# Moving transposes and row statistics of V, K, Q, HGRN input and convolution further behind their producers in a two-layer hybrid trunk

## The chip, the core and the metric

The kernel runs on one core of a Trainium2 chip. The metric is the device time of one execution in microseconds (us); a result is the median of several executions. The engines are named as in the profile: PE is the matrix engine (PEld is its weight load), DVE the vector engine, ACT the scalar engine, POOL the general-purpose engine, SP the engine whose queue issues the transfers.

## The reference, cut to what matters

```
for l in range(2):
    h = rms_norm(x, norm_mix[l])
    z = h @ w_in[l]                                   # 20 blocks of 128 columns
    q_a, k_a, v_a, q_h, i_h, f_fw, f_bw, g_h, a_c, g_c = split(z)
    q_a, k_a = rope(rms_norm(q_a, q_norm[l])), rope(rms_norm(k_a, k_norm[l]))
    o_att = block_attention(q_a, k_a, v_a)            # 8 query heads, 2 key heads of 64
    o_hg  = hgrn2_bidirectional(q_h, i_h, f_fw, f_bw, g_h, ...)
    o_cv  = conformer_conv(a_c, g_c, ...)             # GLU, 31 taps, layer norm, swish
    x = x + concat(o_att, o_hg, o_cv) @ w_out[l]
    x = x + square(relu(rms_norm(x) @ w1[l])) @ w2[l]
```

All is float32, 1024 tokens of 1024 features.

## The kernel before, in words

Activations lie with features on the partitions and the 1024 tokens along the row. A dense product of one block of 128 output columns ("a column" below) is made in `dense_steps` (L214): eight steps over the input blocks, each of six matmuls of 128x512 (three passes of a split into a high and a low part, for two halves of the tokens). The columns come in the order of ZORDER. A column's result stands in a pair of PSUM banks, the tile S, of which there are two; smaller results go to banks `c` and `e`, two of each. `evac` (L316) multiplies the result by the row's 1/rms into SBUF on DVE.

A layer goes through these stages:

1. The four convolution columns, then five columns for HGRN half 0: `Hgrn(0)` computes gates and, last, the input `iv` from column 8, which it transposes on PE at once (L438 to L445, into the tile `vt`).
2. `h0.core()` (L510), the recurrence of half 0 as a generator: `near` (L447), one multiplication, then for six levels `scores` (L476) and a multiplication, then the transposes of K into `Kt` (L532), the states `U` (L545), the outputs `o` (L562) and the output norm. It has 29 yields. At each yield the loop at L702 draws `qg, cg, qg, cg`: two steps of `qkv` (the six columns V, K, Q0 to Q3) and two steps of `conv_all`, whose 60 taps are single DVE instructions (L352), 30 for each of two halves, with `conv_tail` (L366) behind them.
3. `Hgrn(1)` with five more columns; between them it draws three more steps of the convolution, and ahead of its last column it makes the scores of the first two attention units. `drain(cg)` ends the convolution.
4. 64 attention units (the loop over `u`, L828): scores into S, scaling and row extreme on DVE (L756), exponential on ACT (L759), the normalisation on POOL (L761), eight transposes on PE (L782), a copy on ACT (L786) and a subtraction on DVE (L787) for each half, and the products with V (L803). `h1.core()`, the recurrence of half 1, is drawn once every second unit. When it is exhausted, the mixed results are read back and split (L205, L206).
5. The output columns, then the two MLP products, each made of seven block products with fewer multiplications.

The parts of `qkv`: `vpart` evacuates V, and after its yield makes eight transposes (L637). `kpart` evacuates K and squares it; after its yield come the row sums on PE (`tok_sums`, L162), a reciprocal root on DVE (`rstd`), a spread to full rows on ACT (`widen`, L168), the rotary steps (`rope`), eight transposes of the spread factors (`flip`, L178), two multiplications (L660) and the store to `kd`. `qpart` squares and scales on ACT straight from S and does the rest, up to the store to `qd`, after its yield. The rest of each part is run when the next column is at its third step:

```
                for k, _ in enumerate(zsteps(col, lambda zp: start(part(zp)))):
                    if k == 2 and rest:
                        drain(rest.pop(0))
                    yield
```

`conv_tail` has two halves, a mean and a variance; each is a chain of `tok_sums`, `widen`, `flip` and four multiplications or subtractions on DVE (L379, L394), and it ends with a scaling on POOL (L397), a sigmoid on ACT (L398), a product on POOL (L399) and the store.

What sets the order: every engine has its own queue, which it works through in order. The framework fills the queues when it compiles: the order of the program is the priority, and an instruction that its model of the times holds for not ready is passed by later ones that are. A `yield` therefore gives the work that is drawn at that place the precedence over what stands behind the yield. Tiles of one tag share a fixed number of buffers, and the next tile waits for the release of an old one: `x8` has 8, `tmp` has 4, `X` and `T` of the HGRN one each (`Kt` takes the buffer of `T`), `m4` five.

Of the kernel before, what the change touches and what calls it, by code (L numbers as in the profile page):

```python
# [17 lines left out]
P = 128  # L18
# [27 lines left out]
def tile_hybrid_trunk(  # L46
# [223 lines left out]
    def drain(gen):  # L270
        for _ in gen:
            pass
# [14 lines left out]
    for l in range(DEPTH):  # L287
# [78 lines left out]
        def conv_tail(ys):  # L366
# [5 lines left out]
            mc = cst.t([P, 8], "mc", bufs=2)  # L372
            nc.vector.tensor_copy(mc, sp[:, 0:8])
            w = widen(mc, 1)
            for h in range(2):
                b = flip(w, h)
                for y in ys:
                    sl = y[:, h * 512 : (h + 1) * 512]
                    nc.vector.tensor_tensor(sl, sl, b, op=ALU.subtract)  # L379
# [7 lines left out]
            sp = pse()  # L387
            tok_sums(sp, sq[0], mean_w)
            w = widen(rstd(sp[:, 0:8], 8, 1.0), 1)
            for h in range(2):  # L390
                b = flip(w, h)
                for y in ys:
                    sl = y[:, h * 512 : (h + 1) * 512]
                    nc.vector.tensor_tensor(sl, sl, b, op=ALU.mult)  # L394
# [7 lines left out]
        class Hgrn:  # L402
            def __init__(self, ls, mid=lambda: None):
# [31 lines left out]
                mid()  # L435
                iv = self.iv = hg.t([P, L], "m4", bufs=5)
                evac(ztile(8 + ls), iv)
                for h in range(2):  # L438
                    tpv = pse()
                    for q in range(4):  # L440
                        c = h * 4 + q
                        nc.tensor.transpose(tpv[:, q * P : (q + 1) * P], iv[:, c * P : (c + 1) * P], ident)
                    nc.scalar.activation(
                        vt[:, h * 4 : h * 4 + 4, :], tpv.rearrange("p (a b) -> p a b", a=4), AF.Copy
                    )  # L445

            def near(self):  # L447
                X, w0, iv = self.X, self.hks, self.iv
# [3 lines left out]
                for hf in range(2):  # L452
# [2 lines left out]
                        op=ALU.mult,  # L455
                    )
                yield
                t = tmp()
                for h in range(2):
                    sl = slice(h * 512, (h + 1) * 512)  # L460
# [49 lines left out]
            def core(self):  # L510
# [23 lines left out]
                for d in range(2):  # L534
                    for g in range(2):
                        tk = psc()
                        for q in range(4):
                            c = g * 4 + q
                            nc.tensor.transpose(tk[:, q * P : (q + 1) * P], X[:, 3 * d, c * P : (c + 1) * P], ident)
                        nc.scalar.activation(  # L540
                            Kt[:, d, g * 4 : g * 4 + 4, :], tk.rearrange("p (a b) -> p a b", a=4), AF.Copy
                        )
                    yield
                for d in range(2):
                    U = pse()  # L545
                    for c in range(8):
# [100 lines left out]
        def kpart(zp):  # L647
# [5 lines left out]
            sp = pse()  # L653
            tok_sums(sp, sq, hsel)
            krw = widen(rstd(sp[:, 0:16], 16, 1.0 / 64), 2)
            nc.gpsimd.tensor_scalar(kz, kz, pv(l, "kn"), 0.0, op0=ALU.mult, op1=ALU.add)
            rope(kz)
            for h in range(2):
                sl = kz[:, h * 512 : (h + 1) * 512]
                nc.vector.tensor_tensor(sl, sl, flip(krw, h), op=ALU.mult)  # L660
# [26 lines left out]
        def qkv():  # L687
            rest = []

            def start(part):  # L690
                rest.append(part)
                next(part)

            for col, part in [(5, vpart), (4, kpart)] + [(j, lambda zp, j=j: qpart(zp, j)) for j in range(4)]:
                for k, _ in enumerate(zsteps(col, lambda zp: start(part(zp)))):
                    if k == 2 and rest:
                        drain(rest.pop(0))
                    yield
            drain(rest.pop(0))

        qg = qkv()
        for _ in h0.core():  # L702
# [125 lines left out]
        for u in range(NU):  # L828
# [5 lines left out]
            if u >= 2:  # L834
                att_values(u // 2 - 1, u % 2)
            att_flip(u, 1)
            if gen is not None and u % 2 == 0:
                try:
                    next(gen)
                except StopIteration:  # L840
# [443 lines left out]
```

## Time and profile before

| | |
|---|---|
| median of 3 runs | 2546.32 us (2542.85 to 2547.26) |
| the profiled execution | 2548.54 us |
| its span in the profile | 2546.8 us |
| PE busy | 2451.1 us, 96% |
| DVE busy | 2003.2 us, 79% |
| ACT busy | 1202.9 us, 47% |
| POOL busy | 779.0 us, 31% |

The profiled execution is 2.22 us over the median, and its span is 1.74 us shorter than its own time. In the views below, the timeline gives start, duration, engine, line, operation, output <- input, and in square brackets how long the engine had been idle and which instruction ended the wait. "x4" merges four instructions in a row. A table of windows gives for each stretch of the span the busy time of each engine and in brackets the number of instructions. The view of waits gives, for an engine and a line, the sum, the number and the longest of its waits for another engine's line.

### The profile page before, as it was taken

The page shows a single profiled execution, that of the slowest core. Times are in us where ns is not written, and L with a number is a line of the kernel's source. Part 1 is how long each engine was busy: PE and PEld are TensorE (multiplying, and loading weights), DVE is VectorE, ACT ScalarE, POOL GpSimd, SP SyncE. Part 2 cuts the span into 40 slices and gives each one's busy share as a digit, 9 for nine tenths or more (in the row PEclk, how much of TensorE's full clock was granted, in tenths as well). Part 3 has the DMA queues.
Part 4 walks back from the last instruction along what each step waited for, and adds up shares of the span by engine and source line. Part 5 has one row for each costly group of instructions (what it writes and reads, how often), then busy time and mean ns, then how long its engine had stood idle before and what let it go on. Part 6 is the DMA issues. An engine that isn't in the chain of part 4 may idle for free.

```text
span 2546.8 us, 34055 instructions
## 1 busy us (share of the span) xinstructions
PE 2451.1 (96%) x12608; PEld 2020.0 (79%) x12608; DVE 2003.2 (79%) x3023; ACT 1202.9 (47%) x1960; POOL 779.0 (31%) x491
## 2 busy tenths in 40 slices
PE   8989999999999999999999899999999999999999
PEld 7767778878778887888887777888787888878887
DVE  5998598872887777987859985898639877789876
ACT  4222478863544443443423225787635444444332
POOL 0232566433154430000123325664331544200000
PEclk9999999999999999999999999999999999999999
DMA  4101310032244448454221113000322444574442
GB/s 157 60 25 63 103 35 18 14 124 96 83 168 158 148 166 302 162 175 152 69 106 50 42 63 104 18 18 26 133 90 95 163 143 167 191 260 155 162 155 91
DMA packets 113077, 286.99 MB, mean 113 GB/s; under 512 B 11408, under 2 KB 11664, under 8 KB 112912
## 3 DMA queue, kind: packets, MB, share of 16 engines
q1 hardware_dynamic: 112912, 284.83, 32.2%
q8 instruction: 99, 1.62, 0.3%
q14 instruction: 66, 0.54, 0.1%
HBM read 197.75 MB, written 87.03 MB: 112 GB/s over the span
## 4 chain that ended last, share of the span: by engine, by line
PE 77%; DVE 14%; ACT 3%; issue 2%; POOL 2%; DMA 1%; SPq 0%; DVEq 0%; ACTq 0%; POOLq 0%
PE S L223 15%; PE S L1195 10%; PE c L995 9%; PE e L1195 7%; PE c L1195 6%; PE e L995 6%; PE S L995 6%; DVE x L352 4%; PE e L803 4%; PE c L782 3%; PE S L745 3%; PE e L494 2%; PE e L162 1%; PE e L583 1%; DVE P L756 1%
## 5 line engine op out<-in xcount | busy, mean ns | idle before, releaser
L223 PE MATMUL S<-xs,whi 128*128 128x512 f32 x1280 | 363.7, 405 | 10.4 <-ACT xs L208 8.9
L223 PEld LDWEIGHTS S<-xs,whi 128*128 128x128 f32 x1280 | 243.3, 193 | 66.2 <-ACT xs L208 8.9
L223 PE MATMUL S<-xs,wlo 128*128 128x512 f32 x640 | 203.3, 398 | 0.0
L1195 PE MATMUL S<-xs,xs 128*128 128x512 f32 x816 | 201.2, 390 | 0.3 <-DVE xs L897 0.3
L896 ACT ACTIVATE xs<-m 128x512 fp32r<-128x512 f32 x216 | 126.0, 619 | 157.4 <-DVE m L907 52.3
L761 POOL TENSOR_SCALAR P<-P,mx 128x1024 f32<-128x1024 f32 x124 | 142.4, 1149 | 162.8 <-DVE mx L760 125.3
L787 DVE TENSOR_TENSOR PT<-c,PT 128x512 fp32r<-128x512 f32 x256 | 171.1, 684 | 23.0 <-ACT PT L786 21.5
L786 ACT ACTIVATE PT<-c 128x512 fp32r<-128x512 f32 x256 | 147.3, 593 | 67.7 <-PE c L782 64.2
L1195 PEld LDWEIGHTS S<-xs,xs 128*128 128x128 f32 x816 | 153.1, 188 | 32.8 <-DVE xs L897 1.2
L199 ACT ACTIVATE whi<-raw 128x1024 fp32r<-128x1024 f32 x56 | 59.1, 1058 | 245.9 <-PE S L223 232.8
L803 PE MATMUL e<-PT,x 128*128 128x256 f32 x1024 | 172.3, 298 | 0.8 <-ACT PT L786 0.5
L756 DVE TENSOR_SCALAR_CACHE_REDUCE P<-S,nqc 128x1024 f32<-128x1024 f32 x124 | 158.6, 1279 | 13.9 <-PE S L745 8.7
L352 DVE SCALAR_TENSOR_TENSOR x<-x,par,x 128x1009 f32<-128x1009 f32 (+14 forms) x120 | 166.7, 1390 | 1.8
L897 DVE TENSOR_TENSOR xs<-m,xs 128x512 fp32r<-128x512 f32 x216 | 144.9, 694 | 24.8 <-ACT xs L896 24.8
L260 POOL TENSOR_TENSOR tmp<-tmp,tmp 128x1024 f32<-128x1024 f32 x19 | 50.6, 2664 | 364.4 <-ACT tmp L259 364.2
L782 PE MATMUL c<-cons,P 128*128 128x128 f32 x992 | 151.9, 277 | 10.5 <-POOL P L761 5.6
L745 PE MATMUL S<-x,QS 128*128 128x512 f32 x480 | 153.8, 419 | 4.9 <-DVE P L756 4.6
L759 ACT ACTIVATE P<-P,mx 128x1024 f32<-128x1024 f32 x124 | 142.5, 1149 | 24.6 <-DVE P L756 23.3
L1195 PE MATMUL e<-xs,xs 128*128 128x512 f32 x552 | 142.9, 395 | 7.2 <-ACT xs L896 6.8
L803 PEld LDWEIGHTS e<-PT,x 128*128 128x128 f32 x1024 | 138.9, 193 | 8.5 <-ACT PT L786 2.2
L782 PEld LDWEIGHTS c<-cons,P 128*128 128x128 f32 x992 | 115.1, 141 | 36.7 <-issue 10.4
L223 PEld LDWEIGHTS S<-xs,wlo 128*128 128x128 f32 x640 | 122.4, 192 | 26.6 <-issue 0.3
(310 smaller groups left out, 5679.3 us busy)
## 6 DMA issues: line engine op xcount, KB each, us to landing
m<-ad SPq DMA_DIRECT2D x104, 512.0 KB, 3.8
ad<-x SPq DMA_DIRECT2D x176, 256.0 KB, 2.1
raw<-w_in_t SPq DMA_DIRECT2D x40, 512.0 KB, 3.3
xs<-w_t SPq DMA_DIRECT2D x36, 512.0 KB, 3.8
raw<-w_t SPq DMA_DIRECT2D x36, 512.0 KB, 3.6
m<-w_t SPq DMA_DIRECT2D x32, 512.0 KB, 6.3
ad<-tmp SPq DMA_DIRECT2D x48, 256.0 KB, 2.2
x<-w_t SPq DMA_DIRECT2D x24, 512.0 KB, 4.8
```

The lines of the kernel that those rows point to most:

```text
L223: nc.tensor.matmul(zp[h] if type(zp) is list else zp[:, h, :], w, xx[:, h * 512 : (h + 1) * 512], start=first, stop=last)
L352: nc.vector.scalar_tensor_tensor(y[:, lo:hi], u[:, lo + d : hi + d], par[:, l, wof + tap : wof + tap + 1], y[:, lo:hi], op0=ALU.mult, op1= ...
L745: nc.tensor.matmul(S[:, hb, :], qs, kk[:, hb * 512 : (hb + 1) * 512], start=first, stop=not first)
L756: nc.vector.tensor_scalar(Pt, S, nqc[:, j, ci : ci + 1], 3.0e38, op0=ALU.mult, op1=ALU.min, accum_out=mx[:, 1:2])
L759: nc.scalar.activation(Pt, Pt, AF.Exp, bias=mx[:, 1:2], scale=-1.0, accum_out=mx[:, 2:3])
L782: nc.tensor.transpose(t[:, q * P : (q + 1) * P], Pt[:, hb, q * P : (q + 1) * P], ident)
L786: nc.scalar.activation(hi, src, AF.Copy)
L787: nc.vector.tensor_tensor(lo, src, hi.bitcast(F32), op=ALU.subtract)
L803: nc.tensor.matmul(pvp[:, cs], VS[g][:, hb * 4 + kb, :], pt[:, kb, :], start=hb == 0 and n == 0, stop=hb == 1 and n == 7,)
L897: ordered("v", nc.vector.tensor_tensor(lo, src, hi.bitcast(F32), op=ALU.subtract))
L995: nc.tensor.matmul(bank, w[i][:, kt * P : (kt + 1) * P], BC[name][kt][j], start=n == 0 and name not in ("M6", "M7", "M3"), stop=n == 11, s ...
L1195: nc.tensor.matmul(banks[dt], w[i][:, dt * P : (dt + 1) * P], a[j], start=n == 0 and name not in ("M6", "M7", "M3"), stop=n == 3 * SG - 1, ...
```

## The change

Six edits, all of the place at which instructions stand in the program; the arithmetic is the same.

- The transposes of `iv` leave the constructor of `Hgrn` and become a generator `turned`, which `near` runs behind two yields, with a yield behind each half. `near` has 6 yields in place of 3. This holds for both halves of the HGRN.
- In the core, the yield behind the transposes into `Kt` stands behind each group of four and not behind two groups: 4 yields in place of 2. The core has 34 yields in all.
- `conv_tail` yields 4 times between `widen` and `flip` of the mean, and 6 times between those of the variance.
- `kpart` has two more yields: ahead of the scaling and rotary steps, and ahead of the transposes.
- `qkv` no longer drains the rest of a part at the third step of the next column. It resumes it once at the seventh step; K, in the column Q0, at the third and fifth; and at every step while two parts are open, which is how the last third of K runs at the first step of Q1.
- The attention loop draws from `h1.core()` at every unit up to 13, and at every second one from 14 on.

```
@@ conv_tail
             w = widen(mc, 1)
+            for _ in range(4):
+                yield
             for h in range(2):
                 b = flip(w, h)
...
             w = widen(rstd(sp[:, 0:8], 8, 1.0), 1)
+            for _ in range(6):
+                yield
             for h in range(2):
                 b = flip(w, h)
@@ Hgrn
                 evac(ztile(8 + ls), iv)
+
+            def turned(self):
                 for h in range(2):
                     tpv = pse()
                     for q in range(4):
                         c = h * 4 + q
-                        nc.tensor.transpose(tpv[:, q * P : (q + 1) * P], iv[:, c * P : (c + 1) * P], ident)
+                        nc.tensor.transpose(tpv[:, q * P : (q + 1) * P], self.iv[:, c * P : (c + 1) * P], ident)
                     nc.scalar.activation(
-                        vt[:, h * 4 : h * 4 + 4, :], tpv.rearrange("p (a b) -> p a b", a=4), AF.Copy
+                        self.vt[:, h * 4 : h * 4 + 4, :], tpv.rearrange("p (a b) -> p a b", a=4), AF.Copy
                     )
+                    yield
@@ near
                 yield
+                yield
+                yield from self.turned()
                 t = tmp()
@@ core
                             Kt[:, d, g * 4 : g * 4 + 4, :], tk.rearrange("p (a b) -> p a b", a=4), AF.Copy
                         )
-                    yield
+                        yield
@@ kpart
             krw = widen(rstd(sp[:, 0:16], 16, 1.0 / 64), 2)
+            yield
             nc.gpsimd.tensor_scalar(kz, kz, pv(l, "kn"), 0.0, op0=ALU.mult, op1=ALU.add)
             rope(kz)
+            yield
             for h in range(2):
@@ qkv
+            def resume(_=None):
+                if rest and next(rest[0], 1) is not None:
+                    rest.pop(0)
+
             for col, part in [(5, vpart), (4, kpart)] + [(j, lambda zp, j=j: qpart(zp, j)) for j in range(4)]:
                 for k, _ in enumerate(zsteps(col, lambda zp: start(part(zp)))):
-                    if k == 2 and rest:
-                        drain(rest.pop(0))
+                    if len(rest) > 1 or k in ((2, 4) if col == 0 else (6,)):
+                        resume()
                     yield
-            drain(rest.pop(0))
+            while rest:
+                resume()
+                yield
@@ attention loop
-            if gen is not None and u % 2 == 0:
+            if gen is not None and (u % 2 == 0 or u < 14):
```

29 lines of the change are left out of this document (22 added, 7 removed).

## The prediction

> **What bounds the kernel now.** I read the page first, then a table of windows that cuts each layer at the stages the change touches, then PE's view of waits, then the timeline around each wait.
>
> The page:
>
> ```profile
> span 2546.8 us, 34055 instructions
> PE 2451.1 (96%) x12608; PEld 2020.0 (79%) x12608; DVE 2003.2 (79%) x3023; ACT 1202.9 (47%) x1960; POOL 779.0 (31%) x491
> ```
>
> PE is idle for 2546.8 - 2451.1 = 95.7 us. The change leaves PE's work as it is, so all that it can win is part of these idle times, and what is won there counts fully only where PE does not meet the next wait at once. The windows, for layer 0 (HGRN half 0 with V, K, Q; HGRN half 1's columns; the first 15 units or so of the attention; its end) and the first three for layer 1:
>
> ```profile
> 62.00:240.00 178.00, 158.73 (x890) 128.64 (x890) 168.77 (x216) 50.10 (x65) 52.78 (x24) 0.95 0.15 54
> 240.00:317.00 77.00, 74.87 (x419) 60.51 (x418) 44.13 (x78) 28.83 (x32) 33.82 (x16) 0.98 0.26 86
> 317.00:372.00 55.00, 49.16 (x316) 40.27 (x313) 52.21 (x92) 42.59 (x76) 36.79 (x26) 1.00 0.14 44
> 540.00:572.00 32.00, 28.61 (x171) 23.62 (x169) 23.22 (x42) 23.65 (x35) 9.29 (x8) 0.95 0.55 194
> 1327.00:1505.00 178.00, 162.91 (x892) 131.28 (x892) 167.49 (x217) 49.98 (x65) 54.71 (x24) 0.93 0.15 51
> 1505.00:1582.00 77.00, 73.79 (x421) 59.52 (x419) 46.96 (x78) 29.45 (x33) 35.16 (x15) 1.00 0.27 87
> 1582.00:1637.00 55.00, 49.97 (x312) 41.47 (x312) 51.06 (x89) 41.34 (x74) 35.50 (x27) 0.97 0.14 43
> ```
>
> The columns are the window, its length, and busy PE, PEld, DVE, ACT, POOL. In the first stage PE idles 178 - 158.73 = 19.3 us in layer 0 and 15.1 us in layer 1, while DVE idles only 9.2 and 10.5 us: DVE is the fuller engine there. In the second stage PE is nearly full and DVE has 32.9 and 30.0 us to spare. At the start of the attention both are near full: PE idles 5.8 and 5.0 us, DVE 2.8 and 3.9 us.
>
> PE's waits, of both layers together (sum, number, longest):
>
> ```profile
> PE e L442 <- DVE m L322: 11.1, 4, 4.3
> PE e L637 <- DVE A L501: 9.8, 2, 6.2
> PE e L178 <- ACT tmp L168: 7.2, 5, 2.8
> PE c L539 <- ACT T L540: 6.1, 2, 3.1
> PE e L494 <- DVE tmp L660: 4.1, 2, 2.1
> PE e L162 <- DVE A L505: 3.3, 2, 2.3
> ```
>
> These six rows are 41.6 us, and they are the transposes and sums that the change moves, or neighbours of them on the two `e` banks. Two in the timeline, the transposes of `iv` and those of V:
>
> ```profile
> 105.92 10.59 DVE L352 SCALAR_TENSOR_TENSOR x<-x,par,x 128x1017 f32<-128x1017 f32 x6
> 106.05 3.40 POOL L432 TENSOR_TENSOR tmp<-tmp,tmp 128x1024 f32<-128x1024 f32 x1 [4.70 <-ACT tmp L429]
> 113.04 0.39 PE L223 MATMUL S<-xs,whi 128*128 128x512 f32 x1
> 116.43 1.22 DVE L322 TENSOR_TENSOR m<-S,Rb 128x1024 f32<-128x1024 f32 x1
> 117.70 1.33 PE L442 MATMUL e<-cons,m 128*128 128x128 f32 x8 [4.27 <-DVE m L322]
> 126.17 1.26 DVE L352 SCALAR_TENSOR_TENSOR x<-x,par,x 128x1011 f32<-128x1011 f32 x1
> 145.50 1.27 DVE L501 TENSOR_TENSOR A<-e,masks 128x512 f32<-128x512 f32 x2
> 146.23 1.97 PE L637 MATMUL e<-cons,tmp 128*128 128x128 f32 x8 [6.23 <-DVE A L501]
> ```
>
> The evacuation of column 8 stands in DVE's queue behind six taps, which took 10.59 / 6 = 1.77 us each beside POOL's product, against 1.26 us for a tap alone. PE had issued one matmul of the next column and then stood 4.27 us at its transposes. The order in the queue thus supposes a DVE that is faster than the real one, and every PE instruction that is placed shortly behind its DVE producer pays the lag. The second row is of another sort: V itself was ready, and PE waited for an `e` bank that the masking of the scores held.
>
> **The change part by part.** A step of a column takes, from the start of one to the start of the next:
>
> ```profile
> 262.25 1.07 PE L223 MATMUL S<-xs,whi 128*128 128x512 f32 x4
> 263.61 1.07 PE L223 MATMUL S<-xs,whi 128*128 128x512 f32 x4
> ```
>
> 1.36 us. So two yields of the core (four steps) put 5.4 us of PE work between the evacuation of `iv` and its transposes; the sums and transposes of V and Q come four steps later, also 5.4 us; those of K a whole column later.
>
> `iv`, 11.1 us: 5.4 us covers the longest wait of 4.27, and in half 1 the transposes go into the third and fourth unit of the attention, behind the matmuls of two units. I take all of it. If the cover failed, the wait would come back in full.
>
> `Kt`, 6.1 us: the buffer of `T` is released late and both `c` banks are full; with a yield between the groups, PE has other work there. I take all.
>
> L178, 7.2 us: K's factors move behind a column, but the longest waits, up to 2.8, belong also to HGRN's output norm, which is not moved. Half: 3.6.
>
> The three rows on `e` banks, 9.8 + 4.1 + 3.3 = 17.2 us: the transposes still need a bank that DVE has to free, only at another place, where it may again be held. Between nothing and all I take half, 8.6.
>
> The clock: the same eight transposes without a long wait ahead take
>
> ```profile
> 319.19 1.09 PE L442 MATMUL e<-cons,m 128*128 128x128 f32 x8 [1.85 <-DVE m L322]
> 1383.16 1.97 PE L442 MATMUL e<-cons,m 128*128 128x128 f32 x8 [4.27 <-DVE m L322]
> ```
>
> 1.09 us, against 1.33 and 1.97 behind 4.27 and 1.97 behind 6.23. Without the waits 0.24 + 0.88 + 0.88 = 2.0 us go too. The Trainium skill, page "TensorE: Matmul & The Clock Gate", section "What's actually happening", has the array at half clock for about 3.4 us after an idle window of that length; an estimate by it would be 1.7 us for each of the four waits over 3.4, or 6.8 in place of 2.0. The 1.33 us row agrees only in part; the sum keeps 2.0.
>
> Gain so far: 11.1 + 6.1 + 3.6 + 8.6 + 2.0 = 31.4 us.
>
> Can DVE let PE have it? The core now has five yields more, ten steps, so up to 13.6 us more column work stands ahead of its tail, and PE can run on into half 1's columns, where DVE has its 30 us to spare. That is the cover for a DVE that is not faster than before.
>
> Costs. First, the attention. In units 0 to 13 the core is drawn 14 times, not 7; six of these are `near`, so at unit 13 it is four draws ahead: three halves of scores and a multiplication. By
>
> ```profile
> L505 DVE COPY_PREDICATED A<-masks,e 128x512 f32<-128x512 uint8 x20 | 14.8, 740 | 2.5 <-PE e L494 2.4
> L525 DVE TENSOR_TENSOR X<-X,T 128x512 f32<-128x512 f32 x14 | 12.4, 885 | 0.0
> ```
>
> that is 6 x 0.74 + 2 x 0.885 = 6.2 us of DVE work, in a window where DVE idles 2.8 and 3.9 us: 3.4 + 2.3 = 5.7 us for both layers. Later units are lightened by as much, but there PE is the bound.
>
> Second, the convolution's end. Of `conv_all`'s 72 yields `h0.core()` now draws 68 and `Hgrn(1)` three, so the last piece of `conv_tail` falls to `drain(cg)`, behind the exponentials of units 0 and 1 and just ahead of the attention. Its rows now:
>
> ```profile
> 295.25 2.48 DVE L394 TENSOR_TENSOR x<-x,e 128x512 f32<-128x512 f32 x4 [1.91 <-PE e L178]
> 297.31 4.39 POOL L397 TENSOR_SCALAR x<-x,par 128x1024 f32<-128x1024 f32 x2 [5.82 <-DVE x L394]
> 301.68 2.40 POOL L399 TENSOR_TENSOR tmp<-tmp,x 128x1024 f32<-128x1024 f32 x1
> 304.71 1.28 ACT L431 ACT_TABLE_LOAD   x1
> 306.01 0.20 ACT L431 ACTIVATE mx<-tmp 128x1 f32<-128x1 f32 x1
> ```
>
> On DVE 2.5 us a layer, in full: 5.0. On ACT the sigmoid now stands between exponentials, so at least two table loads more, 2 x 1.28 = 2.6 us a layer (four, 5.1, if an exponential slips between the two sigmoids); ACT idles 55 - 42.6 = 12.4 us there, so half: 2.6 for both. On POOL 4.39 + 2 x 2.40 = 9.2 us a layer, which L761 of units 2 and 3 may have to stand behind; POOL idles 18.2 us there. Between 0 and 9.2 I take 1: 2.0. The Trainium skill, page "ScalarE: Activation LUTs", section "What ACT_TABLE_LOAD costs", prices a switch at about 2.66 us, load and drain. The trace has 1.28 and the next instruction 0.02 us behind it, so no drain shows; by the page the sum would be 2.8 us worse.
>
> Costs: 5.7 + 5.0 + 2.6 + 2.0 = 15.3 us.
>
> The end of the attention: the core is exhausted at unit 54, not 58, and the mixed results are split four units earlier. PE idles 32 - 28.6 = 3.4 us there in layer 0, and I suppose as much in layer 1. Half goes: 3.4 us for both layers, between 0 and 6.8.
>
> The stores move too: K's goes to SP's queue a column later, and is first read here,
>
> ```profile
> 189.61 1.27 DVE L660 TENSOR_TENSOR tmp<-tmp,e 128x512 f32<-128x512 f32 x2
> 266.31 0.45 SPq L713 DMA_DIRECT2D tmp<-kd  x1
> ```
>
> 75 us after its last multiplication; a column of 8 x 1.36 = 10.9 us is hidden. Q's stores, 5.4 us later, are read unit by unit: nothing.
>
> Sum: 2548.5 - 31.4 + 15.3 - 3.4 = 2529.0 us on the scale of the profiled execution, which is 2.2 us over the median of the runs. Forecast 2526.8 us.
>
> **The rivals.** *DVE decides, and the waits only move* (no change). PE cannot win in the first stage more than DVE can give up: its idle 9.2 + 10.5 = 19.7 us, less what is not PE's fault, as here,
>
> ```profile
> 139.35 0.67 DVE L526 TENSOR_TENSOR T<-T 128x256 f32<-128x256 f32 x1 [2.42 <-POOL X L525]
> ```
>
> twice 2.4: 14.9 us. Then 2548.5 - 14.9 + 15.3 - 2.2 = 2546.7. For it speaks the 95% of DVE, against it DVE's idle stage right behind. The change not doing what it says belongs here: the queue passes instructions that it holds for not ready, and a yield then moves nothing; the row at 113.04 shows such passing.
>
> *The convolution's end blocks the attention* (slower). Its `y` tiles hold the two `x8` buffers that the second pair of key tiles needs. DVE waits for that split already now,
>
> ```profile
> 315.88 2.13 DVE L206 TENSOR_TENSOR x<-tmp,x 128x1024 fp32r<-128x1024 f32 x1 [7.20 <-POOL x L761]
> ```
>
> while PE still has a column to do. If it stands there with no column left, all the attention's DVE work is behind it in the queue, for the chain 2.48 + 4.39 + 2.56 (loads) + 2 x 3.40 (POOL's products beside a busy DVE) + 2.13 = 18.4 us a layer. The sum has 2.5 + 1.3 + 1.0 = 4.8 of it, so 27.2 us more: 2554.0. It decides if more than about 12 us a layer are exposed beyond those 4.8.
>
> *More goes than I count* (faster): all of the `e` banks' 8.6, L178's 3.6, and half of the costs, 7.6: 19.8 us less, 2507.0.
>
> **How the numbers follow.** About 0.2%, 5.1 us, is what a measurement of this kernel tells from no change: 2541.2 to 2551.4. Forecast 0.56, more 0.10, DVE decides 0.18, blocked attention 0.16. So faster 0.66, same 0.18, slower 0.16. The range reaches from the third rival's 2507 to the second's 2554.
>
> **What would show it.** Right: the rows of L442 and L539 gone from PE's waits, PE idle under 10 us in each first stage, L525's and L494's rows of half 0 ending later against the columns of Q; two to four table loads more a layer; a fuller DVE in the first 55 us of the attention, with L782 or L745 waiting more. Wrong: new waits of PE for DVE of 3 us or more in the first stage that add up to what has gone; or a wait of DVE at L206 ahead of unit 2 of over 12 us with PE idle beside it.

## The result, and the profile after

The changed kernel takes 2564.77 us (median, 2564.02 to 2565.44), the kernel before 2544.97 us beside it on the same chip. The ratio is 1.0072, 95% interval 1.006 to 1.0085: slower by 0.72%, or 18 us (the two medians are 19.8 us apart; the text goes by the ratio). The forecast was 2526.8, and the measured time lies above the range.

The page of the changed kernel, and its span and mean granted clock:

```profile
span 2563.2 us, 34056 instructions
PE 2467.0 (96%) x12608; PEld 2026.6 (79%) x12608; DVE 1992.3 (78%) x3023; ACT 1207.0 (47%) x1964; POOL 757.8 (30%) x491
```
```profile
core 0: 2563.2 us, clock 0.983
```

PE idles 2563.2 - 2467.0 = 96.2 us, and it was 95.7. As much waiting as the change removes has thus come back elsewhere. What has grown is PE's *busy* time, by 15.9 us for the same 12608 matmuls. The clock says most of why: the kernel before had a mean of

```profile
core 0: 2546.8 us, clock 0.988
```

so the time lost to a lower clock was 0.012 x 2546.8 = 30.6 us and is now 0.017 x 2563.2 = 43.6 us: at most 13 of the 15.9. PE stands idle for a part of its time at half clock. Where it is busy, half clock covers 53.6 us of the trace before and 71.9 us of the trace after, and half of the difference is 9.1 us. The rest of the 15.9 isn't explained. The third digit of the clock isn't firm either: over its executions in all runs the kernel before shows 0.984 to 0.989, the changed one 0.981 to 0.983.

The waits of PE in the changed kernel, both layers (line numbers behind L378 are up to 17 higher than before: L442 is now L448, L462 is L471, L471 is L480, L745 is L762, L786 is L803, L803 is L820):

```profile
PE e L820 <- ACT PT L803: 13.7, 4, 6.7
PE e L480 <- DVE tmp L473: 10.7, 2, 5.8
PE e L178 <- ACT tmp L168: 7.9, 6, 2.4
PE S L762 <- POOL QS L752: 6.3, 2, 3.2
PE e L162 <- POOL tmp L368: 5.2, 2, 2.6
PE e L471 <- ACT vt L449: 3.2, 2, 1.9
PE S L223 <- DVE x L773: 2.6, 2, 1.3
PE e L448 <- DVE m L322: 0.8, 2, 0.4
```

The `iv` transposes wait 0.8 us in place of 11.1, and the rows of V's transposes (9.8) and of `Kt` (6.1) are gone. In their place stand L820, at the start of the attention; L480 and L471, `near`'s products right behind the `iv` transposes; L762, the last query; and L162 and L223 around the convolution's end and half 1's columns.

The table of windows. The work comes later than before (unit 3 of the attention by 2.9 us in layer 0, the first tap of layer 1 by 9.0 us and its unit 3 by 11.9), so the windows of the attention and of layer 1 are shifted by as much, to begin at the same work:

```profile
62.00:240.00 178.00, 167.25 (x919) 133.89 (x918) 165.30 (x201) 49.36 (x65) 48.71 (x24) 0.95 0.16 55
240.00:317.00 77.00, 71.10 (x382) 55.58 (x381) 44.79 (x92) 27.57 (x29) 27.31 (x14) 0.93 0.22 72
319.90:374.90 55.00, 47.69 (x295) 39.39 (x294) 47.66 (x85) 40.53 (x71) 34.71 (x26) 0.91 0.16 49
1336.00:1514.00 178.00, 168.85 (x923) 134.95 (x922) 166.12 (x203) 49.47 (x65) 49.17 (x25) 0.95 0.15 51
1514.00:1591.00 77.00, 70.81 (x379) 55.87 (x378) 43.63 (x89) 27.58 (x29) 27.52 (x14) 0.93 0.22 72
1593.90:1648.90 55.00, 47.60 (x295) 39.11 (x294) 47.76 (x86) 40.54 (x71) 34.22 (x25) 0.91 0.18 51
```

In the first stage PE is busy for 8.5 and 5.9 us more than before, so something was won there. Half 1's columns then give back 3.8 us in layer 0 (71.10 against 74.87, clock 0.93 against 0.98) and 3.0 in layer 1 (clock 0.93 against 1.00). At the start of the attention PE has 295 matmuls in each layer where it had 316 and 312, and the clock falls from 1.00 and 0.97 to 0.91. DVE is emptier there than before, 47.66 and 47.76 us against 52.21 and 51.06.

Differences of start times in the two traces (first tap of the convolution, scaling of attention units 3, 16, 32, 56 and 63, last output column) give the change of each stage's length in us:

| stage | layer 0 | layer 1 |
|---|---|---|
| first tap to unit 3 | +2.5 | +3.0 |
| units 3 to 16 | +9.9 | +8.5 |
| units 16 to 32 | -5.1 | -5.1 |
| units 32 to 56 | +3.0 | +3.1 |
| units 56 to 63 | +7.4 | +7.2 |
| unit 63 to the last output column | -7.1 | -7.3 |

Drawing half 1 earlier moves work from units 16 to 32 into units 3 to 16, and drawing the output columns earlier moves work to the left of unit 63. These pairs should cancel. The first pair costs 3 to 5 us a layer more than it returns. In all the two layers lose 20.0 us here, and the rest of the span is 3.6 us shorter.

**The first stage.** The timeline of the changed kernel around `near`'s products:

```profile
126.53 3.91 DVE L534 TENSOR_TENSOR X<-X,T 128x512 f32<-128x512 f32 x2
126.66 1.98 PE L471 MATMUL e<-m,cons 128*128 128x512 f32 x4 [1.89 <-ACT vt L449]
131.34 2.56 DVE L352 SCALAR_TENSOR_TENSOR x<-x,par,x 128x1010 f32<-128x1010 f32 x2
134.95 1.41 DVE L473 TENSOR_TENSOR tmp<-e,m 128x256 f32<-128x256 f32 x4
135.85 3.75 PE L480 MATMUL e<-m,cons 128*128 128x512 f32 x4 [5.84 <-DVE tmp L473]
```

PE makes the product `d1` (L471) at 126.66. Its readers on DVE (L473) come only at 134.95, behind a multiplication of 3.91 us, two taps and more. The banks stay full until then, and the next product, `d0` (L480), waits 5.84 us for one. The old wait at the transposes was 4.27.

**The start of the attention:**

```profile
311.62 0.45 SPq L730 DMA_DIRECT2D tmp<-kd  x1
315.36 4.77 POOL L403 TENSOR_TENSOR tmp<-tmp,x 128x1024 f32<-128x1024 f32 x2
317.79 2.68 SPq L404 DMA_DIRECT2D mixd<-tmp  x2
320.52 0.45 SPq L731 DMA_DIRECT2D tmp<-kd  x1
320.59 0.09 DVE L773 DVE_READ_ACCUMULATOR P<-S,nqc 128x1 f32 x1
324.52 1.06 ACT L205 ACTIVATE x<-tmp 128x1024 fp32r<-128x1024 f32 x1 [3.84 <-DMA tmp<-kd]
325.60 1.28 ACT L776 ACT_TABLE_LOAD   x1
326.89 1.15 ACT L776 ACTIVATE P<-P,mx 128x1024 f32<-128x1024 f32 x1
329.19 0.58 PE L820 MATMUL e<-PT,x 128*128 128x256 f32 x1 [6.60 <-ACT PT L803]
```

This chain is read from the bottom. PE waits 6.60 us for ACT's copy of a transposed unit (L803). In ACT's queue that copy stands behind the exponential at 326.89, whose input was complete at 320.68 (320.59 + 0.09), but which stands behind L205, the split of the second key pair. L205 idles ACT for 3.84 us until the key's DMA lands. That DMA was issued at 320.52, because SP's queue first held the convolution's two stores (L404), which had to wait for POOL's products of 4.77 us. The other half of the same key had been issued at 311.62 (L730), so its buffer was free long before; only the order of the queue held the second half back. The Trainium skill, page "TensorE: Matmul & The Clock Gate", section "Architectural detail: the array is 16× 32×32, not 1× 128×128", has ACT and DVE work their queues strictly in order; the wait of a ready exponential behind an unready split agrees.

**The end:** the copy of the last query comes late, beside four splits of mixed results that now fall into units 54 to 57.

```profile
555.13 1.26 POOL L752 TENSOR_TENSOR QS<-tmp,QS 64x512 fp32r<-64x512 f32 x1
556.44 3.69 PE L762 MATMUL S<-x,QS 128*128 128x512 f32 x8 [3.23 <-POOL QS L752]
```

### The profile page after: what moved, and what is told of

Read it like the earlier page. It is cut to its first block, busy times and chain, and to the rows that moved or that the text cites. A ratio compares the mean times of both kernels' runs of the same rounds, so it can differ in the third digit from the quotient of the medians.

```text
span 2563.2 us, 34056 instructions
## 1 busy us (share of the span) xinstructions
PE 2467.0 (96%) x12608; PEld 2026.6 (79%) x12608; DVE 1992.3 (78%) x3023; ACT 1207.0 (47%) x1964; POOL 757.8 (30%) x491
## 5 line engine op out<-in xcount | busy, mean ns | idle before, releaser
L223 PE MATMUL S<-xs,whi 128*128 128x512 f32 x1280 | 367.1, 407 | 11.5 <-ACT xs L208 8.8
L223 PEld LDWEIGHTS S<-xs,whi 128*128 128x128 f32 x1280 | 243.4, 194 | 68.9 <-ACT xs L208 8.8
L223 PE MATMUL S<-xs,wlo 128*128 128x512 f32 x640 | 202.8, 398 | 0.0
L803 ACT ACTIVATE PT<-c 128x512 fp32r<-128x512 f32 x256 | 148.0, 593 | 92.7 <-PE c L799 90.5
L820 PE MATMUL e<-PT,x 128*128 128x256 f32 x1024 | 169.5, 299 | 14.3 <-ACT PT L803 13.7
L773 DVE TENSOR_SCALAR_CACHE_REDUCE P<-S,nqc 128x1024 f32<-128x1024 f32 x124 | 158.6, 1279 | 29.9 <-PE S L762 20.7
L352 DVE SCALAR_TENSOR_TENSOR x<-x,par,x 128x1009 f32<-128x1009 f32 (+14 forms) x120 | 173.3, 1444 | 1.6
L762 PE MATMUL S<-x,QS 128*128 128x512 f32 x480 | 152.4, 427 | 10.4 <-POOL QS L752 6.3
L820 PEld LDWEIGHTS e<-PT,x 128*128 128x128 f32 x1024 | 138.1, 194 | 21.2 <-ACT PT L803 15.1
L223 PEld LDWEIGHTS S<-xs,wlo 128*128 128x128 f32 x640 | 123.0, 193 | 26.0
```

What stands on the lines that cost most here:

```text
L223: nc.tensor.matmul(zp[h] if type(zp) is list else zp[:, h, :], w, xx[:, h * 512 : (h + 1) * 512], start=first, stop=last)
L352: nc.vector.scalar_tensor_tensor(y[:, lo:hi], u[:, lo + d : hi + d], par[:, l, wof + tap : wof + tap + 1], y[:, lo:hi], op0=ALU.mult, op1= ...
L762: nc.tensor.matmul(S[:, hb, :], qs, kk[:, hb * 512 : (hb + 1) * 512], start=first, stop=not first)
L773: nc.vector.tensor_scalar(Pt, S, nqc[:, j, ci : ci + 1], 3.0e38, op0=ALU.mult, op1=ALU.min, accum_out=mx[:, 1:2])
L803: nc.scalar.activation(hi, src, AF.Copy)
L820: nc.tensor.matmul(pvp[:, cs], VS[g][:, hb * 4 + kb, :], pt[:, kb, :], start=hb == 0 and n == 0, stop=hb == 1 and n == 7,)
```

## The experiments

The theory at this point had three costs: first-stage waits that only move, the convolution's end in front of the attention, and the pace of half 1's core. The rival was that one of them alone explains the 18 us. Every time below is a median with the ratio to the kernel before on the same chip; that one took 2546.7 to 2550.2 us.

**Undoing parts of the change.** tail_undone takes out the ten yields in the convolution's end:

```
-            for _ in range(4):
-                yield
...
-            for _ in range(6):
-                yield
```

> The changed kernel without the ten yields in the convolution's end; the other five edits stay. Queue theory: the loss sits at the start of the attention, where the late stores of the convolution stand ahead of the second key load in SP's queue, and ACT's and DVE's queues stand at the split of these keys. In each layer that costs a wait of 6.6 us and up to 5 us of half clock behind it, so this kernel takes 2542 to 2550 us and the wait is gone. Pacing theory: the loss is the core drawn at every unit up to 13; then it stays at 2560 or more. Spacing theory: the loss is in the stage ahead of the attention; then it also stays at 2560 or more.

Measured: 2557.41 us, ratio 1.0039 (1.0024 to 1.0054). The window at the start of the attention, shifted with unit 3 as above, shows it:

```profile
318.90:373.90 55.00, 49.97 (x316) 41.16 (x315) 50.87 (x86) 39.78 (x70) 36.17 (x25) 0.97 0.10 30
```

PE has 316 matmuls and a clock of 0.97 there again, and the wait of 6.6 us is gone. The yields in the convolution's end cost 0.33%, 8.4 us. That is less than half of the loss, and the time is above the 2542 to 2550 us that were expected.

end58 draws from half 1 at every unit only below 10 (`u < 10` for `u < 14`), so that the core ends at unit 58 as before.

> The changed kernel with the core drawn at every unit up to 9, not 13, so that it is exhausted at unit 58, as before the change, and not at unit 54. Collision theory: at unit 54 the read-back of the mixed results meets the last query's load and split; that costs some 5 us in each layer between units 56 and 63, so this kernel takes 2553 to 2557 us. If the end of the core does not matter: 2563 to 2566 us. If the pace of units 10 to 13 matters by itself, units 8 to 16 become shorter by 2 us or more a layer.

Measured: 2562.41 us, 1.0053 (1.0038 to 1.0068). The whole is worth 0.2%, about 5 us, less than was expected and not clear of noise, since the intervals overlap. The wait at L762 for POOL's copy is gone. From unit 56 to the last output column each layer is 1.2 us shorter than in the changed kernel, so the collision at the last query is worth about half of the 5 us; the rest goes with the draws at units 11 and 13, which come later here.

keys_late makes the second key pair at unit 6, not ahead of the attention:

```
-        keys(1)
...
         for u in range(NU):
+            if u == 6:
+                keys(1)
```

> The changed kernel with the second pair of key tiles loaded and split at unit 6 and not ahead of unit 0 (they are first needed at unit 30). The convolution's end stays late. Queue theory: the wait of 6.6 us ahead of the first product with V goes, with its half clock: 2543 to 2552 us. If the work of the convolution's end on DVE, POOL and ACT is what delays units 2 and 3, and not the order of the queues, the wait stays and the kernel takes 2560 us or more.

Measured: 2574.25 us, 1.0099 (1.0084 to 1.0114), a miss. The wait of 6.6 went, but a wait of 3.56 us at L762 came, for the scaling of a unit (L773) on DVE, which stood behind a subtraction of the query (L752) that took 3.50 us beside POOL's work. The key's work then fell into the attention, where PE's waits at L762 for L773 add up to 17.5 us in place of 3.9.

store_pool issues the convolution's two stores from POOL's queue (`nc.gpsimd.dma_start` for `nc.sync.dma_start` at L404).

> The changed kernel with the two stores of the convolution's end issued from POOL's queue and not from SP's. Queue theory: these stores wait for POOL's products and hold back the second key load and the query loads behind them on SP; without them the loads go out some 8 us earlier, the wait of 6.6 us ahead of the first product with V goes, and the kernel takes 2550 to 2558 us. If the order on SP is not the cause, the wait stays and so does the time, 2563 to 2567 us.

Measured: 2588.04 us, 1.0162 (1.0147 to 1.0177), a miss by far. The second half of the key was issued at 312.46 in place of 320.52 and the wait of 6.6 us went, as the theory had it. A wait of 5.85 us at L762 took its place; ahead of its end DVE works through the key's split (L206), the query's subtraction (L752, 2.72 us) and a unit's scaling (L773), one behind the other from 321.61 to 326.90. The whole costs 23 us more than the change itself. Most of it is clock: by the mean of 0.976 up to 0.024 x 2588.5 = 62.1 us are lost, against 43.6 in the changed kernel, while PE idles 101.8 us against 96.2. What brings the clock down is left open.

**One part alone, on the kernel before.** kvq_only makes the edits to `kpart` and `qkv` and nothing else.

> The kernel before with one edit: K, V and Q are resumed later (the yields in K, and the later steps in which the parts are resumed). If more distance pays in the first stage: 2535 to 2541 us, with the waits of PE for the transposes of V and of K's factors gone. If the waits only move, because DVE is full there: 2542 to 2548 us. If the spacing itself costs: 2550 us or more.

Measured: 2539.94 us, 0.9965 (0.9951 to 0.9979): faster by 9 us. V's row of 9.8 us is gone from PE's waits. PE idles 74.5 us (2535.0 - 2460.5) in place of 95.7, but its busy time has grown by 9.4, so less than the idle time that went was won. These rows stay:

```profile
PE e L442 <- DVE m L322: 11.2, 4, 4.3
PE e L178 <- ACT tmp L168: 7.3, 6, 2.2
```

turned_only moves the `iv` transposes with their yields and draws at units 1, 3 and 5 as well (`u % 2 == 0 or u < 6`).

> The kernel before with one edit: the transposes of the HGRN input run inside near, behind two yields, with a yield behind each half; the core is drawn at the odd units 1, 3 and 5 too, so that it still ends at unit 58. Theory that this edit is the loss of the first stage: the wait for these transposes (4.3 us in each layer) goes, and in its place PE waits for DVE at the next products of near, 4 to 6 us with half clock behind it; 2550 to 2560 us. If near's spacing is neutral and the loss comes from an edit that acts together with others: 2540 to 2549 us.

Measured: 2566.94 us, 1.0079 (1.0064 to 1.0094), more than was expected. This one part alone costs 20 us. By start times, the loss lies ahead of unit 3: 9.4 and 10.7 us in the two layers. Units 3 to 16 are only 0.4 us longer in each, so the draws at units 1, 3 and 5 aren't the cause. Its waits (L476 is `d0`, L499 the scores, L656 the squaring of K):

```profile
PE e L476 <- DVE tmp L469: 10.7, 2, 5.8
PE S L223 <- DVE tmp L322: 6.7, 2, 3.3
PE c L499 <- ACT m L487: 6.3, 2, 3.2
PE e L162 <- ACT tmp L656: 6.1, 2, 3.6
PE e L162 <- DVE A L510: 5.3, 4, 1.4
```

kt_only has the yield behind each group of `Kt`, and draws at units 1 and 3 (`u < 4`).

> The kernel before with one edit: a yield behind each group of four transposes of K in the core; the core is drawn at units 1 and 3 too, so that it ends at unit 58. If distance pays here: the waits of 3.0 and 3.1 us go, 2538 to 2543 us. If they only move: 2543 to 2549 us.

Measured: 2566.43 us, 1.0073 (1.0057 to 1.009), a miss.

pace54 changes no order in the core; it puts five empty yields ahead of half 1's core and draws at every unit below 14.

```
+                for _ in range(5 if ls == 1 else 0):
+                    yield
```

> The kernel before with the new pace alone: half 1's core has five empty yields at its start and is drawn at every unit up to 13, so that it ends at unit 54; nothing ahead of the attention is changed. Pacing theory: this costs 3 us or more a layer, partly in units 3 to 16 by a fuller DVE, partly behind unit 48 by the earlier read-back: 2551 to 2558 us. If the pace is neutral: 2542 to 2548 us.

Measured: 2555.01 us, 1.0033 (1.002 to 1.0046), as expected. By start times units 3 to 16 are 9.7 and 9.6 us longer than before and units 16 to 32 5.0 us shorter, much as in the changed kernel. The scores of a unit wait for a DVE that is behind:

```profile
355.16 0.76 PE L747 MATMUL S<-x,QS 128*128 128x512 f32 x1 [4.52 <-DVE P L758]
```

**Is it the yield at Kt or its two draws?** kt_mid is kt_only with the two draws at units 25 and 41.

> The kernel before with a yield behind each group of Kt's transposes, as in kt_only, but the two draws that half 1 needs more are put at units 25 and 41, not at 1 and 3. Theory 'the pace at the start is the cost': the loss of units 3 to 16 (kt_only 20 us a layer against 10 to 12 before) is gone, PE's waits at L539 stay gone, and the time is 2540-2548. Rival 'the yield itself is the cost': units 3 to 16 don't matter, the first stage of layer 0 loses 5 us more than before, and the time stays above 2556.

Measured: 2550.83 us, 1.0012 (1.0003 to 1.0021), above the 2540 to 2548 that were expected. The first of the two rows is kt_only, the second kt_mid, for the 55 us from unit 3 of layer 0:

```profile
329.37:384.37 55.00, 49.15 (x290) 40.48 (x290) 46.72 (x82) 35.91 (x63) 32.17 (x25) 0.91 0.06 17
```
```profile
320.94:375.94 55.00, 51.22 (x327) 42.98 (x325) 49.80 (x91) 42.76 (x76) 38.56 (x29) 0.97 0.07 19
```

With the same yield, 37 matmuls more fit into the window. The two kernels are 15.6 us apart, and not all of that is shown to be the draws. From unit 3 to unit 63 kt_only takes 6.6 and 5.6 us more in the two layers, 12.2 together. But in layer 0 it is 8.4 us behind already at unit 3, although up to 329 us both programs have the same instructions in the same order on every engine. The same sums on PE waited 3.25 us at 240.40 in kt_only and 1.36 us at 239.49 in kt_mid, and then one ran at half clock for 10 us and the other at full clock:

```profile
239.60:249.80 10.20, 9.40 (x43) 7.17 (x43) 7.35 (x17) 0.00 (x0) 2.35 (x1) 0.50 0.13 46
```
```profile
239.60:249.80 10.20, 10.20 (x107) 7.13 (x107) 9.67 (x14) 0.00 (x0) 2.39 (x1) 1.00 0.20 70
```

As a whole the yield gains nothing, although the wait at L539 is gone: from the first tap to unit 3 kt_mid is 4.5 and 0.9 us shorter than the kernel before, and units 32 to 56, where one of the two draws now stands, are 3.4 us longer in each layer.

after_mid does the same to the whole change: its five draws more are at units 21, 27, 33, 39 and 45.

> The changed kernel, with the five draws that half 1's core needs more than before put at units 21, 27, 33, 39 and 45, not at the odd units below 14. Theory 'the pace costs': units 3 to 16 lose 11 to 12 us a layer in place of 15, the core ends at unit 58 as before and the end loses 9 in place of 14; units 16 to 32 give back 3: 4 to 6 us a layer, 2553-2558. Rival 'what is late at the start is the end of the convolution alone': the wait of 6.6 at the values stays and with it the time, 2561-2567.

Measured: 2557.11 us, 1.004 (1.0027 to 1.0053). The pace costs 0.32%, 8 us, in the whole change. This holds the end of the core at unit 54 too, since after_mid ends at unit 58; against end58, which does so as well, the place of the five draws is worth 0.13%, 3 us, and is not clear of noise.

**Why do the iv transposes cost 20 us?** First theory: DVE is full and lags. light_before and light_turned leave out every second tap of the convolution (30 of 60 a layer), in the kernel before and in turned_only:

```
+                if tap % 2:
+                    yield
+                    continue
```

> The kernel before, but every second tap of the convolution is left out (30 of 60 DVE instructions a layer; the convolution's result is thus another one), its yields kept. It is the base for light_turned. 30 x 1.26 = 38 us of DVE work a layer are gone, nearly all of it from the first stage, where PE waits. Theory 'DVE lags': PE's waits for DVE there (L442 11.1, L637 9.8, L494 4.1) fall to under 8 us together and the time to 2525-2538. Rival 'order of the banks' (the waits come from where the instructions stand, however idle DVE is): more than 15 us of these waits stay and the time is 2540-2546.

> light_before with the iv transposes moved as in the change (turned, six near yields, a draw at every unit below 6). Beside its own base, light_before. Theory 'DVE lags': the new waits of turned_only (PE 5.8 and 4.9 us at the product d0 of near for a bank, 3.1-3.3 at the scores) were DVE's lag and are gone, each under 2 us; the time is light_before's within 4 us. Rival 'order of the banks': the two yields let the e banks be held by other work and the waits of 3-6 us stay; light_before's time plus 12 to 20 us.

Measured: 2521.4 us, 0.9889 (0.9874 to 0.9904), and 2539.78 us, 0.9968 (0.9956 to 0.9979). Without half of the taps the wait at the `iv` transposes is 1.5 us and the kernel 27 us faster, so the time of the first stage does hang on DVE. But light_turned is still 18.4 us behind its own base. The two rows of its waits:

```profile
PE e L162 <- ACT tmp L659: 7.3, 2, 3.6
PE e L479 <- DVE tmp L472: 1.6, 2, 0.8
```

The wait at `d0` (here L479) is down to 0.8 us, as the theory had it. Others are there without the taps too: L659 is the squaring of K, for which its sums wait 3.6 us, and the scores still wait up to 3.1. The theory of a full DVE falls.

Second theory: the yields use up the columns and the core's end stands bare. turned_spread is turned_only with

```
-        for _ in h0.core():
-            for g in (qg, cg, qg, cg):
+        for i, _ in enumerate(h0.core()):
+            for g in ((qg, cg, qg, cg) if i < 17 else (qg, cg, cg)):
```

> turned_only, but h0.core() draws two column steps of qkv only at its first 17 yields and one at the last 15: 34 + 15 = 49 steps, so that the columns last to the core's end; the six yields of near and the levels up to there are as in turned_only. Theory 'the cover is spent': the three yields more in near use up six column steps, and the end of the core (with two steps at each of 32 yields the 49 steps are gone at the 25th) stands bare; turned_only loses what it loses there, behind about 170 us of the stage's PE work. Then most of that is back: 2545-2554. Rival 'the banks': the loss is the new waits for e banks at near's products, whatever the columns do: 2560-2568 as turned_only.

Measured: 2585.05 us, 1.0147 (1.0134 to 1.0161). It is some 17 us slower still, with new waits of 4.9 us at the sums of a Q and 5.0 at the scores. This theory falls as well.

Third: what matters is what the three yields draw. shift3 leaves the transposes where they were and puts three empty yields behind `near`'s first one, in half 0 alone; shift3_cols draws only column steps at these three.

```
-                yield
+                for _ in range(1 if self.ls else 4):
+                    yield
```

> The kernel before with three empty yields behind near's first yield, in half 0 alone; the iv transposes stay where they were, half 1 and its pace too. So the core draws as in turned_only: six column steps ahead of its products, and 64 of the convolution's 72 yields instead of 58, whose last pieces (its mean) thus come into the core's end. Theory 'the draws': turned_only's loss came from what its three yields draw, not from the place of the transposes: 2558-2568, with the iv wait of 4.3 still there. Rival 'the transposes' place': without moving them the yields cost under 5 us: 2543-2552.

> shift3, but its three yields draw two column steps each and no tap of the convolution, so that the convolution stands against the core as before (58 yields) and only the columns are six steps ahead. If the columns' shift is what costs: within 5 us of shift3. If the earlier taps and the convolution's mean in the core's end cost: within 5 us of the kernel before, 2543-2552, and the waits behind 200 us (L162, L223) as before.

Measured: 2569.46 us, 1.0085 (1.007 to 1.01), and 2570.38 us, 1.008 (1.0061 to 1.01). Nothing but six column steps drawn earlier against the core costs what turned_only costs. The waits of shift3:

```profile
PE e L442 <- DVE m L322: 8.5, 2, 4.3
PE e L162 <- ACT tmp L652: 7.3, 2, 3.6
PE S L223 <- DVE tmp L322: 6.7, 2, 3.3
PE c L495 <- ACT m L483: 6.0, 2, 3.0
```

L652 is again the squaring of K, L495 the scores. The last three are turned_only's rows, with the `iv` transposes in their old place and still waiting 4.3. So it is the alignment of the columns with the core: each column brings an evacuation, sums and transposes, which now meet other pieces of the recurrence. Which of the meetings costs most isn't separated.

The loss is hardly idle time of PE. In shift3 PE idles 98.5 us (2568.5 - 2470.0) and in shift3_cols 98.1 (2568.4 - 2470.3), against 95.7 before, but its busy time is 18.9 and 19.2 us longer for the same matmuls. The mean clocks are 0.982 and 0.980 against 0.988, which by the same reckoning as above is up to 15.6 and 20.8 us. So the meetings cost mostly through the clock behind them, and the rows of waits show where, not how much.

kvq_turn1 tells the same from the other side: kvq_only with the `iv` transposes one yield later, directly behind `near`'s first, and no yield more.

> kvq_only with the iv transposes only behind near's first yield, one draw behind their evacuation (2.7 us of PE work), without further yields and with the pace of before. Theory: the wait of 4.27 at the iv transposes falls to about 1.5 in each layer, no instruction of near comes later than before, so no new wait at the bank of d1 and d0: 4 to 6 us under kvq_only, 2533-2537. Rival: behind near's products DVE lags by as much, the wait moves on to L471 or L480: 2539-2546.

Measured: 2540.13 us, 0.9968 (0.9956 to 0.9981): the same as kvq_only's 0.9965. Moved without a shift of the columns, the transposes cost nothing and gain nothing; their longest wait is 3.1 us in place of 4.3.

**Two attempts at a better version.** turn1_spread is kvq_turn1 with one column step at the last nine yields of the core.

> kvq_turn1 (its core has 29 yields) with two column steps at the first 20 yields and one at the last nine. Theory 'the cover is spent': the kernel before has the same bare end (49 steps are gone at the 25th of 29 yields), so there is something to win on any version: 3 to 8 us under kvq_turn1, 2532-2537. Rival: the columns of half 1 cover the end already, as the queue passes waiting work; then nothing or a little loss, 2539-2546.

Measured: 2544.38 us, 0.9984 (0.9973 to 0.9995), 4 us above kvq_turn1, though the intervals overlap. after_mended is the whole change without the yields in the convolution's end, with the five draws in the middle and the columns spread.

> The changed kernel with what the runs point to: no yields in the convolution's end, the five draws in the middle of the attention, two column steps at the first 17 yields of half 0's core and one at the last 17. By the pieces, V, K and Q's spacing -9, the iv move about 0 with its cover, Kt 0 as in kt_mid: 2535-2543. If the pieces hinder one another on the e banks: 2545-2555.

Measured: 2592.75 us, 1.0179 (1.0166 to 1.0192), with a wait of 8.9 us at the output norm's sums of half 0: its square on ACT stands until the convolution's store releases a `tmp` buffer. Spreading the columns hurt clearly in turned_spread; in turn1_spread the loss isn't clear of noise, and after_mended has no counterpart without it. The best kernels of the study are kvq_only and kvq_turn1, alike within the noise.

## Why the prediction was wrong, point by point

The failed step is the gain, 31.4 us: it was counted row by row, with "PE can run on into half 1's columns" as the cover. In the traces the stretch from the first tap to unit 3, where nearly all of this gain should stand, is 2.5 and 3.0 us longer than before. The costs, 15.3 us, look nearly right: 8.4 for the convolution's end and 8 for the pace, 16.4 together. But this is in part luck: the 8 us hold the end of the attention, which was forecast as a gain of 3.4, and the path of the 8.4 was another one. That the two add up without remainder wasn't tried by itself; if they do, 18.3 - 16.4 = 1.9 us of loss is left for the place where 31.4 us of gain were forecast. The parts tried alone don't add up: -9 (V, K, Q), +20 (`iv`) and +3 (`Kt`, kt_mid) with these 16.4 would be 30 us. So how much of the `iv` move's 20 us is in the whole change stays open.

- *iv, 11.1, "I take all of it".* The row went, and 10.7 + 3.2 us came at the next two products of the same chain, for banks and for `vt`. The step took PE's wait for a cost of the place. It was the lag of a chain of DVE and ACT work behind it. The price of the cover, six column steps ahead of the core, was put at nothing; alone it is 20 us (shift3_cols).
- *Kt, 6.1, all.* The row went, and the time did not fall: 1.0012 with the draws in the middle (kt_mid).
- *L178, half of 7.2.* 7.9 us: nothing.
- *e banks, half of 17.2.* For V, K and Q alone the size was right: kvq_only gains 9 us, against the 8.6 forecast here. That is luck in part, since PE's idle time fell by 21.2 us and its busy time rose by 9.4. In the whole change it is outweighed.
- *Clock, a gain of 2.0.* A loss of 9 us where PE is busy, and of at most 13: the removed waits took their half-clock stretches along, and the new ones brought more.
- *The pace of half 1's core, 5.7.* 8 us, with the core's earlier end in it. The sign that was named for it, a fuller DVE in the first 55 us of the attention, is wrong: DVE is emptier by 4.6 and 3.3 us. So the cost isn't a DVE that is full; that it is what waits in order behind the core's work is argued, not shown.
- *The convolution's end, 5.0 + 2.6 + 2.0 = 9.6.* 8.4 us measured. ACT executes four instructions more, two table loads a layer, as forecast. But the path was another, so the near figure is luck: SP's queue and the split of the key on ACT, not DVE, ACT and POOL work.
- *The end of the attention, a gain of 3.4.* Nothing: units 56 to 63 lose 7.4 and the output columns return 7.1 in layer 0; the collision at the last query costs some 2.4 us in both layers together (end58).

Of the rivals, "the waits only move" was right for the gains, but it kept 14.9 us of them as what DVE can give up; light_turned shows that the waits move with half of the taps gone too. "The convolution's end blocks the attention" was right in its place. Its mechanism, DVE at L206 behind the `x8` buffers, did not occur: L206 waits 2.67 us. The sign for "wrong" that was named first, a new wait of PE for DVE of 3 us or more in the first stage, is the one that showed: 5.84 us, and 4.87 in layer 1.

## What to carry to other kernels

A row in the list of PE's waits isn't a price: where a chain of DVE and ACT work is late, the wait removed at one consumer comes back at the next one, and only a run of that part alone tells the gain. The idle time of PE isn't the price either: compare its busy time and its mean clock as well, for here PE idled 96.2 us against 95.7 and the loss stood in its busy time. A yield in a generator that others are drawn against isn't free: it shifts all that is drawn at later yields, and here three empty ones cost as much as the whole change. When a change has several parts, run each alone and each at another place of its draws; here one part (V, K, Q) gained 9 us, and two others lost through draws that they didn't need where they were put. And compare two traces in windows that begin at the same work: a layer that starts 9 us later fills a fixed window with other work.

## What the runs showed of the hardware

A short wait can halve the clock. The same eight transposes, first before, then in the changed kernel:

```profile
180.31 1.10 PE L178 MATMUL e<-cons,tmp 128*128 128x128 f32 x8 [1.30 <-ACT tmp L168]
```
```profile
174.32 1.97 PE L178 MATMUL e<-cons,tmp 128*128 128x128 f32 x8 [2.39 <-ACT tmp L168]
```

Behind 1.30 us they take 1.10, behind 2.39 us 1.97. The granted clock of the 3.4 us around the second was

```profile
174.10:177.50 3.40, 3.18 (x12) 2.89 (x13) 3.40 (x5) 2.20 (x3) 1.85 (x1) 0.51 0.46 154
```

0.51. The Trainium skill, page "TensorE: Matmul & The Clock Gate", section "What's actually happening", has half clock begin after about 3.4 us of idle time; here a gap of 2.39 us was enough. The length of the wait doesn't decide alone, however. In the kernel before, PE stood still for 3.03 us, and the 3.4 us behind that ran at full clock:

```profile
222.34 0.93 PE L539 MATMUL c<-cons,X 128*128 128x128 f32 x6 [3.03 <-ACT T L540]
```
```profile
222.34:225.74 3.40, 3.40 (x19) 2.92 (x20) 3.40 (x8) 2.41 (x4) 0.32 (x1) 1.00 0.43 154
```

And in the changed kernel 6.8 us at half clock follow 3.4 us in which PE was busy throughout, so not every such stretch stands behind a wait:

```profile
187.84:191.25 3.41, 3.41 (x27) 3.23 (x26) 3.41 (x5) 0.00 (x0) 2.09 (x2) 1.00 0.00 0
191.25:198.08 6.83, 6.83 (x21) 5.10 (x20) 4.54 (x9) 1.85 (x2) 0.00 (x0) 0.50 0.32 118
```

So a new wait of 2.4 us can cost 1.7 us more than itself (half of 3.4), but need not, and the sum of PE's waits doesn't tell what a change of their places does.
